# Convolution taps in a written order beside the query, key and value products of a first layer, on one core

## Chip, core and metric

The kernel runs on one core of one Trainium2 chip. The metric is the device time of one execution in microseconds (us), here the median of several runs; a profiled execution of its own gives the trace.

The engines are named as in the trace: PE is TensorE's matmul, PEld its load of weights, DVE is VectorE, ACT is ScalarE, POOL is GpSimd. DMAs are issued from SP's queue. Every engine works through its own list of instructions in order and waits on semaphores for the others.

## What is computed

The kernel is a chain of four transformer-like layers over 512 positions (and 256 context positions) of width 1024. Only the mixer of the first layer matters here. Cut to that:

```python
def conformer_conv(p_glu, conv_w, conv_b, ln_g, ln_b):
    a, gate = jnp.split(p_glu, 2, axis=-1)
    u = depthwise_conv(a * jax.nn.sigmoid(gate), conv_w, conv_b)   # 31 taps
    return jax.nn.silu(layer_norm(u, ln_g, ln_b))

def even_mixer(...):
    p_lat = h_lat @ w_in
    conv_lat = conformer_conv(p_lat[..., :EV_Q0], conv_w, conv_b, ln_g, ln_b)
    q_lat = apply_axial_rope(qk_heads(p_lat[..., EV_Q0:EV_K0]), rope)
    k_lat = apply_axial_rope(qk_heads(p_lat[..., EV_K0:EV_V0]), rope)
    v_lat = v_heads(p_lat[..., EV_V0:])
    ...
    o = lax.map(lambda qb: diff_attend(qb, k_all, v_all, lam), q_blocks)
    y_lat = jnp.concatenate([conv_lat, diff_merge(o, subln_g, lambda_init)], axis=-1) @ w_out
```

The same is done for the 256 context positions, with one set of weights. Beside it, this stage also computes rows of the modulation `c @ ada_w` for the first layer (kinds 2, 3 and 4) and, before, the filters of a later long convolution (the Hyena filters).

## The kernel before

Data lies with channels on the 128 partitions and positions along the free dimension; 768 columns are 512 latent and 256 context positions. Products run in three passes of rounded halves: `wsplit` (line 60) loads a weight of 128 x 1024 into a buffer `wraw`, ACT rounds it to `whi` (line 73), and a subtraction gives `wlo` (line 74), on VectorE or, where `eng` says so, on POOL. `mm3` (line 87) then adds hi x hi, hi x lo and lo x hi into one PSUM accumulator (lines 90 to 92). `whi` and `wlo` have two buffers each, `wraw` has three.

In `even_mixer` (line 355) the order is this. The input halves of the convolution are made in four channel blocks (`us`, lines 407 to 427), interleaved with the Hyena filters (`fg`). Then comes the stage of the change (lines 436 to 515): eight query and key products (line 489 on), each followed by a rope step of three VectorE passes (`stream_shuffle` line 494, lines 495 and 496) and an addition on POOL (line 497), then the values in two halves of six position tiles (line 501 on). Beside them run the taps of the 31-wide convolution (`taps`, line 437): per channel block 28 `scalar_tensor_tensor` passes of VectorE over 798 columns (line 449), two taps made by ACT (lines 443 and 446) and added on POOL into `o2` (line 447), and one addition of `o2` (line 452) on POOL. `conv_norm` (line 457) normalizes the result in two parts, latent and context. `taps` is a generator; the loops advance it with `next(tg)`.

`mods` (line 141) is a generator too: for each kind eight loads of `ada_w` into `wraw`, each with small products on TensorE (line 153), then a copy of the sum by ACT (line 157, it takes a `wraw` buffer as well) and a transposition (line 160). `behind` (line 168) makes every `wsplit` advance it by n steps, here 2.

Attention follows (line 540 on): 12 units of a head and a block of positions, with `scores` (line 558), `values` (line 590) and, as `filler` (line 623), one output product of the convolution half after each of the first eight units. The other half of the output products follows at the end (line 648).

The instructions of each engine are put in order when the kernel is built, by a planner that takes what is ready, the earlier in the program first; emission order therefore sets priorities and not the order itself. Buffers in one pool rotate; a pool that is opened on the memory of a closed one waits, tile by tile, for the last users of that memory. PSUM has eight banks: `evps` four, `evmps` (modulation) two and, after the filters' `evf` is closed, `evcps` (normalization) two. In attention `evaps`, `evop` and `evgp` lie on the banks of `evps`, and the scores' `evsp` on those of `evmps` and `evcps`.

Of the kernel before, what the change touches and what calls it, by code (L numbers as in the profile page):

```python
# [30 lines left out]
class K:  # L31
# [109 lines left out]
    def mods(self, l, kind, ps, pool=None, bufs=3):  # L141
# [6 lines left out]
        for kt in range(8):  # L148
            w = self.tmp([128, 1024], "wraw", bufs=bufs, pool=pool or self.wp)
            nc.sync.dma_start(out=w, in_=a["ada_w"][l, kt * 128:(kt + 1) * 128, kind * 1024:(kind + 1) * 1024])  # L150
            for hf in range(2):
                j = (kt % 2) * 2 + hf
                nc.tensor.matmul(acc[32 * j:32 * j + 32, :], self.cs[:, kt, :], w[:, hf * 512:(hf + 1) * 512],
                                 start=kt < 2, stop=kt >= 6)
            yield
# [199 lines left out]
def even_mixer(k, xc):  # L355
# [10 lines left out]
    with ExitStack() as es:  # L366
# [4 lines left out]
        mps = hp.enter_context(k.pool("evmps", 2, space=PSUM))  # L371
# [4 lines left out]
        with k.pool("hyf") as hy, k.pool("evf", 2, space=PSUM) as fps:  # L376
            fg = hyena_filters(k, fps, hy)
# [58 lines left out]
        with k.pool("evp") as pp, k.behind([k.mods(0, kind, mps) for kind in (2, 3, 4)], 2):  # L436
            def taps():

                for i in range(4):
# [8 lines left out]
                    for j in range(1, 29):  # L448
                        nc.vector.scalar_tensor_tensor(out=o, in0=u[:, j:j + W], scalar=cw[:, i, j:j + 1], in1=o, op0=ALU.mult, op1=ALU.add)
                        if j == 14:  # L450
                            yield
                    nc.gpsimd.tensor_tensor(out=o, in0=o, in1=o2, op=ALU.add)
# [33 lines left out]
            cps = hp.enter_context(k.pool("evcps", 2, space=PSUM))  # L486
            tg = taps()
            rope = k.cload("rope2d", [128, 2, T], pool=pp)
            for i in range(8):
                w = k.wsplit(a["ev_w_fm"][8 + i], eng=nc.gpsimd if i >= 4 else None)  # L490
                acc = k.gemm(w, h, 8, 0, T, ps)
                t1 = k.tmp([128, T], "rt1", bufs=1, pool=pp)
                t2 = k.tmp([128, T], "rt2", bufs=2, pool=pp)
                nc.vector.stream_shuffle(t2, acc, [(j + 16) % 32 for j in range(32)])
                nc.vector.tensor_tensor(out=t1, in0=acc, in1=rope[:, 0], op=ALU.mult)
                nc.vector.tensor_tensor(out=t2, in0=t2, in1=rope[:, 1], op=ALU.mult)
                nc.gpsimd.tensor_tensor(out=qk[i][:, 0:T], in0=t1, in1=t2, op=ALU.add)
                acc = k.gemm(w, h, 8, T, C, ps)
                nc.scalar.copy(qk[i][:, T:], acc)
                next(tg)  # L500
            for g in range(2):
                vb = [k.wsplit(a["ev_w_v"][g, kq * 4:kq * 4 + 4].rearrange("k p f -> p k f")) for kq in range(2)]
                for t in range(6):
                    acc = k.tmp([128, 512], "acc", pool=ps, bufs=None)[:, :256]
                    for kt in range(8):
                        s = slice(kt % 4 * 256, kt % 4 * 256 + 256)
                        w = vb[kt // 4]
                        k.mm3(acc, (hh[:, kt, t * 128:(t + 1) * 128], hl[:, kt, t * 128:(t + 1) * 128]),
                              (w[0][:, s], w[1][:, s]), kt == 0, kt == 7)
                    s = slice(g * 256, g * 256 + 256)  # L510
                    nc.scalar.copy(vv[:, t, s], acc)
                    if t % 3 == 2:
                        next(tg, None)
# [26 lines left out]
        with k.pool("eva") as pp, k.pool("evaps", 2, space=PSUM) as ps, k.pool("evop", 1, space=PSUM) as op_, k.pool("evgp", 1, space=PSUM) as gp, \  # L540
                k.pool("evsp", 2, space=PSUM) as sp:
# [81 lines left out]
            def filler(u):  # L623
                if u < 8:
                    out_gemm(0, [u], gp)
# [1625 lines left out]
```

## Time and profile before

| | |
|---|---|
| median of 3 runs | 3662.26 us (3659.52 to 3662.49) |
| profiled execution | 3663.87 us |
| its span, first to last instruction | 3662.1 us |
| PE busy | 3421.9 us (93%) |
| DVE busy | 2431.2 us (66%) |
| ACT busy | 1460.6 us (40%) |
| POOL busy | 665.8 us (18%) |

The stage of the change lies between about 170 and 360 us of the span, attention ends near 490. The shares are averages over the whole kernel; the stage differs from them, and it has to be read by itself. An engine's busy time counts what it executes, not whether anyone waits for it; the waits of PE show that. Matmul ends are modelled and overlap, so two matmuls in a row are best read by the distance of their starts.

### The profile page before, as it was taken

How to read it: one execution, taken by the hardware profiler on the slowest of the kernel's cores; microseconds unless marked ns; L12 is line 12 of the kernel's file. 1: busy time of each engine (PE TensorE's matmuls, PEld its weight loads, DVE VectorE, ACT ScalarE, POOL GpSimd, SP SyncE). 2: the span in 40 equal slices, each digit the busy share in tenths (PEclk: the TensorE clock that was granted, in tenths of full speed). 3: DMA queues.
4: the chain of work that ended last, by engine and by line, in shares of the span. 5: the costliest groups of instructions: out<-in, count | busy, mean ns of one | idle time of the engine just before them, and what ended most of it. 6: DMA issues, size and time to landing. Idle time of an engine off the chain costs nothing.

```text
span 3662.1 us, 54926 instructions
## 1 busy us (share of the span) xinstructions
PE 3421.9 (93%) x21924; PEld 2820.3 (77%) x21924; DVE 2431.2 (66%) x3995; ACT 1460.6 (40%) x2525; POOL 665.8 (18%) x587
## 2 busy tenths in 40 slices
PE   6987989999998899889999999999999999999999
PEld 3765878888887667667888877767998877777998
DVE  7997876544458765654334676657877676757886
ACT  4223543222226434323223444543444544644443
POOL 0042101102102332311111032021111032012110
PEclk9997999999999999889999999999999999999999
DMA  6334114333333222332223313232333313232333
GB/s 212 110 120 114 38 52 129 113 123 119 118 102 122 79 76 78 119 103 80 93 92 98 107 58 104 92 121 81 103 105 104 109 50 119 73 132 83 103 98 98
DMA packets 156842, 369.31 MB, mean 101 GB/s; under 512 B 19207, under 2 KB 44167, under 8 KB 156200
## 3 DMA queue, kind: packets, MB, share of 16 engines
q1 hardware_dynamic: 156584, 365.79, 31.5%
q8 instruction: 172, 2.82, 0.3%
q14 instruction: 86, 0.70, 0.1%
HBM read 334.27 MB, written 28.31 MB: 99 GB/s over the span
## 4 chain that ended last, share of the span: by engine, by line
PE 42%; DVE 12%; issue 6%; ACT 4%; POOL 2%; DMA 1%; SPq 0%; DVEq 0%; POOLq 0%; ACTq 0%
PE acc L90 12%; PE acc L92 12%; PE acc L91 12%; DVE wlo L74 1%; DMA wraw<-in_w_up_dram 1%; DVE hb L1614 1%; PE rec L1339 1%; PE rec L1340 1%; ACT whi L73 1%; DVE wslo L85 1%; PE acc L1416 1%; PE acc L1415 1%; DVE oz L830 1%; PE acc L1417 1%; ACT mp L1849 0%
## 5 line engine op out<-in xcount | busy, mean ns | idle before, releaser
L73 ACT CAST whi<-wraw 128x1024 fp32r<-128x1024 f32 (+2 forms) x442 | 408.0, 923 | 862.0 <-PE acc L91 664.4
L74 DVE TENSOR_TENSOR wlo<-wraw,whi 128x1024 fp32r<-128x1024 f32 (+2 forms) x438 | 487.1, 1112 | 185.4 <-ACT whi L73 180.7
L90 PE MATMUL acc<-hh,whi 128*128 128x512 f32 (+1 forms) x1024 | 367.4, 359 | 11.8 <-ACT whi L73 6.4
L92 PE MATMUL acc<-hh,wlo 128*128 128x512 f32 (+1 forms) x1024 | 364.9, 357 | 12.2 <-POOL wlo L74 8.8
L91 PE MATMUL acc<-hl,whi 128*128 128x512 f32 (+1 forms) x1024 | 365.8, 358 | 2.7 <-DVE hl L256 2.3
L91 PE MATMUL acc<-hidl,whi 128*128 128x512 f32 (+1 forms) x768 | 274.2, 357 | 1.6 <-DVE hidl L85 1.6
L92 PE MATMUL acc<-hidh,wlo 128*128 128x512 f32 (+1 forms) x768 | 274.2, 357 | 0.6 <-DVE wlo L74 0.6
L90 PE MATMUL acc<-hidh,whi 128*128 128x512 f32 (+1 forms) x768 | 274.4, 357 | 0.0
L341 POOL TENSOR_TENSOR sqr<-relu 128x512 f32<-128x512 f32 (+1 forms) x96 | 127.8, 1332 | 689.3 <-ACT relu L339 685.8
L90 PEld LDWEIGHTS acc<-hh,whi 128*128 128x128 f32 x1024 | 196.2, 192 | 50.9 <-ACT whi L73 10.2
L92 PEld LDWEIGHTS acc<-hh,wlo 128*128 128x128 f32 x1024 | 195.5, 191 | 47.0 <-POOL wlo L74 10.1
L91 PEld LDWEIGHTS acc<-hl,whi 128*128 128x128 f32 x1024 | 196.9, 192 | 35.4 <-DVE hl L256 5.9
L92 PE MATMUL acc<-shh,wlo 128*128 128x512 f32 (+1 forms) x480 | 194.7, 406 | 7.2 <-DVE wlo L74 7.2
L90 PE MATMUL acc<-shh,whi 128*128 128x512 f32 (+1 forms) x480 | 196.1, 409 | 3.5 <-ACT whi L73 3.5
L91 PE MATMUL acc<-shl,whi 128*128 128x512 f32 (+1 forms) x480 | 194.8, 406 | 1.1 <-issue 1.1
L85 POOL TENSOR_TENSOR flo<-fth,fhi 128x512 fp32r<-128x512 f32 x44 | 82.3, 1870 | 531.4 <-ACT fhi L84 506.5
L90 PE MATMUL acc<-fsh,wshi 128*128 128x256 f32 x576 | 163.7, 284 | 4.4 <-ACT wshi L84 4.4
L91 PEld LDWEIGHTS acc<-hidl,whi 128*128 128x128 f32 x768 | 145.1, 189 | 25.2 <-DVE hidl L85 2.0
L92 PE MATMUL acc<-fsh,wslo 128*128 128x256 f32 x576 | 162.5, 285 | 1.5 <-DVE wslo L85 1.5
L91 PE MATMUL acc<-fsl,wshi 128*128 128x256 f32 x576 | 163.4, 284 | 0.0
L92 PEld LDWEIGHTS acc<-hidh,wlo 128*128 128x128 f32 x768 | 144.3, 188 | 23.9 <-DVE wlo L74 1.0
L191 DVE SCALAR_TENSOR_TENSOR mdacc<-wraw,cs,mdacc 128x1024 f32<-128x1024 f32 x70 | 94.4, 1372 | 102.6 <-DMA wraw<-in_ada_w_dram 102.6
(684 smaller groups left out, 9142.8 us busy)
## 6 DMA issues: line engine op xcount, KB each, us to landing
wraw<-in_mlp_w_dram SPq DMA_DIRECT2D x128, 512.0 KB, 3.5
wraw<-in_ada_w_dram SPq DMA_DIRECT2D x96, 512.0 KB, 4.0
wraw<-in_w_in_dram SPq DMA_DIRECT2D x58, 512.0 KB, 3.5
wraw<-in_od_w_fm_dram SPq DMA_DIRECT2D x36, 512.0 KB, 3.6
wraw<-in_w_gate_dram SPq DMA_DIRECT2D x72, 256.0 KB, 2.9
wraw<-in_w_up_dram SPq DMA_DIRECT2D x72, 256.0 KB, 3.1
wraw<-in_w_down_dram SPq DMA_DIRECT2D x48, 256.0 KB, 2.7
wraw<-in_w_down_dram SPq DMA_DIRECT2D x32, 320.0 KB, 2.9
```

The lines of the kernel that those rows point to most:

```text
L73: nc.scalar.copy(hi, raw)
L74: (eng or nc.vector).tensor_tensor(out=lo, in0=raw, in1=f32(hi), op=ALU.subtract)
L85: (eng or nc.vector).tensor_tensor(out=lo, in0=src, in1=f32(hi), op=ALU.subtract)
L90: nc.tensor.matmul(out, s[0], m[0], start=first, stop=False)
L91: nc.tensor.matmul(out, s[0], m[1], start=False, stop=False)
L92: nc.tensor.matmul(out, s[1], m[0], start=False, stop=last)
L191: nc.vector.scalar_tensor_tensor(out=acc, in0=w, scalar=c, in1=acc, op0=ALU.mult, op1=ALU.add)
L341: nc.gpsimd.tensor_tensor(out=s, in0=r, in1=r, op=ALU.mult)
L830: nc.vector.scalar_tensor_tensor(out=o, in0=p[:, j:j + n], scalar=w[:, j:j + 1], in1=o, op0=ALU.mult, op1=ALU.add)
L1339: nc.tensor.matmul(op_[pf[d], hd], qd[:, c, pf[d]], S[:, c], start=True, stop=False)
L1340: nc.tensor.matmul(op_[pf[d], hd], at[pf[d], c], vn[pf[d], hd], start=False, stop=True)
L1415: nc.tensor.matmul(o, hh[:, kt, ts], w[0][:, ws], start=first, stop=False)
```

## The change

VectorE's instructions in the region of the query, key and value products are issued in the order in which the program emits them (`manual_schedule`); where they fall among VectorE instructions of outside the region, and the order of all other engines, stay the planner's. In the region, 40 steps of `taps` come first (a step is now a single tap, or the addition of `o2`), then the split of the first weight, and for each of the eight products: the next weight's split, five steps, the rope step. Each value tile is followed by three steps. All splits and the additions of `o2` are VectorE's. The normalization comes behind the region. Each `wsplit` advances the modulation by three steps, and three empty steps (`lag`) stand before each kind's copy. The PSUM pools change places: `evcps` is opened first and also serves the modulation before the filters' end, `evmps` is opened on the banks of `evf`; in attention `evsp` is on the banks of `evps`, `evgp` and `evop` on those of `evcps`, `evaps` on those of `evmps`. The convolution's output products come after units 2 to 9 in place of 0 to 7.

```diff
@@ -138,7 +138,7 @@
         nc.vector.tensor_reduce(out=self.sum4, in_=self.ident.rearrange("p (q j) -> p j q", q=4), axis=AX.X, op=ALU.add)
         self.md = {}
 
-    def mods(self, l, kind, ps, pool=None, bufs=3):
+    def mods(self, l, kind, ps, pool=None, bufs=3, lag=0):
 
 
 
@@ -152,6 +152,8 @@
                 j = (kt % 2) * 2 + hf
                 nc.tensor.matmul(acc[32 * j:32 * j + 32, :], self.cs[:, kt, :], w[:, hf * 512:(hf + 1) * 512],
                                  start=kt < 2, stop=kt >= 6)
+            yield
+        for _ in range(lag):
             yield
         row = self.tmp([128, 1024], "wraw", bufs=bufs, pool=pool or self.wp)[:, 0:512]
         nc.scalar.copy(row, acc)
@@ -368,12 +370,13 @@
         cp = es.enter_context(k.pool("evc"))
         tp_ = hp.enter_context(k.pool("evt", side="right"))
         ps = hp.enter_context(k.pool("evps", 4, space=PSUM))
-        mps = hp.enter_context(k.pool("evmps", 2, space=PSUM))
+        cps = hp.enter_context(k.pool("evcps", 2, space=PSUM))
         lam = cp.tile([128, 1], F32, name="lam")
 
         W = TC + 30
         conv = [k.tmp([128, W], "conv", F32, 4, cp) for i in range(4)]
         with k.pool("hyf") as hy, k.pool("evf", 2, space=PSUM) as fps:
+            mps = cps
             fg = hyena_filters(k, fps, hy)
             next(fg)
             xl = load_x()
@@ -433,7 +436,8 @@
             return k.tmp([128, TC], "b3", dt, 8, vp)
 
         qk = [b3() for i in range(8)]
-        with k.pool("evp") as pp, k.behind([k.mods(0, kind, mps) for kind in (2, 3, 4)], 2):
+        mps = hp.enter_context(k.pool("evmps", 2, space=PSUM))
+        with k.pool("evp") as pp, k.behind([k.mods(0, kind, mps, lag=3) for kind in (2, 3, 4)], 3):
             def taps():
 
                 for i in range(4):
@@ -447,9 +451,8 @@
                         nc.gpsimd.tensor_tensor(out=o2, in0=o2, in1=o3, op=ALU.add)
                     for j in range(1, 29):
                         nc.vector.scalar_tensor_tensor(out=o, in0=u[:, j:j + W], scalar=cw[:, i, j:j + 1], in1=o, op0=ALU.mult, op1=ALU.add)
-                        if j == 14:
-                            yield
-                    nc.gpsimd.tensor_tensor(out=o, in0=o, in1=o2, op=ALU.add)
+                        yield
+                    nc.vector.tensor_tensor(out=o, in0=o, in1=o2, op=ALU.add)
                     yield
                 for r in range(2):
                     yield from conv_norm(r)
@@ -483,34 +486,44 @@
                     nc.vector.scalar_tensor_tensor(out=cs[i], in0=th, scalar=1.0, in1=cs[i], op0=ALU.add, op1=ALU.mult)
                 yield
 
-            cps = hp.enter_context(k.pool("evcps", 2, space=PSUM))
             tg = taps()
             rope = k.cload("rope2d", [128, 2, T], pool=pp)
-            for i in range(8):
-                w = k.wsplit(a["ev_w_fm"][8 + i], eng=nc.gpsimd if i >= 4 else None)
-                acc = k.gemm(w, h, 8, 0, T, ps)
-                t1 = k.tmp([128, T], "rt1", bufs=1, pool=pp)
-                t2 = k.tmp([128, T], "rt2", bufs=2, pool=pp)
-                nc.vector.stream_shuffle(t2, acc, [(j + 16) % 32 for j in range(32)])
-                nc.vector.tensor_tensor(out=t1, in0=acc, in1=rope[:, 0], op=ALU.mult)
-                nc.vector.tensor_tensor(out=t2, in0=t2, in1=rope[:, 1], op=ALU.mult)
-                nc.gpsimd.tensor_tensor(out=qk[i][:, 0:T], in0=t1, in1=t2, op=ALU.add)
-                acc = k.gemm(w, h, 8, T, C, ps)
-                nc.scalar.copy(qk[i][:, T:], acc)
-                next(tg)
-            for g in range(2):
-                vb = [k.wsplit(a["ev_w_v"][g, kq * 4:kq * 4 + 4].rearrange("k p f -> p k f")) for kq in range(2)]
-                for t in range(6):
-                    acc = k.tmp([128, 512], "acc", pool=ps, bufs=None)[:, :256]
-                    for kt in range(8):
-                        s = slice(kt % 4 * 256, kt % 4 * 256 + 256)
-                        w = vb[kt // 4]
-                        k.mm3(acc, (hh[:, kt, t * 128:(t + 1) * 128], hl[:, kt, t * 128:(t + 1) * 128]),
-                              (w[0][:, s], w[1][:, s]), kt == 0, kt == 7)
-                    s = slice(g * 256, g * 256 + 256)
-                    nc.scalar.copy(vv[:, t, s], acc)
-                    if t % 3 == 2:
-                        next(tg, None)
+            def some(n):
+                for _ in range(n):
+                    next(tg, None)
+
+
+            with k.tc.manual_schedule(engines={mybir.EngineType.DVE}):
+                some(40)
+                w = k.wsplit(a["ev_w_fm"][8])
+                for i in range(8):
+                    accs = [k.gemm(w, h, 8, c0, n, ps) for c0, n in regs]
+                    if i < 7:
+                        w = k.wsplit(a["ev_w_fm"][9 + i])
+                    else:
+                        vb = [k.wsplit(a["ev_w_v"][0, kq * 4:kq * 4 + 4].rearrange("k p f -> p k f")) for kq in range(2)]
+                    some(5)
+                    acc = accs[0]
+                    t1 = k.tmp([128, T], "rt1", bufs=1, pool=pp)
+                    t2 = k.tmp([128, T], "rt2", bufs=2, pool=pp)
+                    nc.vector.stream_shuffle(t2, acc, [(j + 16) % 32 for j in range(32)])
+                    nc.vector.tensor_tensor(out=t1, in0=acc, in1=rope[:, 0], op=ALU.mult)
+                    nc.vector.tensor_tensor(out=t2, in0=t2, in1=rope[:, 1], op=ALU.mult)
+                    nc.gpsimd.tensor_tensor(out=qk[i][:, 0:T], in0=t1, in1=t2, op=ALU.add)
+                    nc.scalar.copy(qk[i][:, T:], accs[1])
+                for g in range(2):
+                    for t in range(6):
+                        acc = k.tmp([128, 512], "acc", pool=ps, bufs=None)[:, :256]
+                        for kt in range(8):
+                            s = slice(kt % 4 * 256, kt % 4 * 256 + 256)
+                            w = vb[kt // 4]
+                            k.mm3(acc, (hh[:, kt, t * 128:(t + 1) * 128], hl[:, kt, t * 128:(t + 1) * 128]),
+                                  (w[0][:, s], w[1][:, s]), kt == 0, kt == 7)
+                        s = slice(g * 256, g * 256 + 256)
+                        nc.scalar.copy(vv[:, t, s], acc)
+                        some(3)
+                    if g == 0:
+                        vb = [k.wsplit(a["ev_w_v"][1, kq * 4:kq * 4 + 4].rearrange("k p f -> p k f")) for kq in range(2)]
             for _ in tg:
                 pass
 
@@ -537,8 +550,8 @@
                     xs = x[r][:, m]
                     nc.vector.scalar_tensor_tensor(out=xs, in0=acc, scalar=k.mcol(0, 2, r)[:, m:m + 1], in1=xs, op0=ALU.mult, op1=ALU.add)
 
-        with k.pool("eva") as pp, k.pool("evaps", 2, space=PSUM) as ps, k.pool("evop", 1, space=PSUM) as op_, k.pool("evgp", 1, space=PSUM) as gp, \
-                k.pool("evsp", 2, space=PSUM) as sp:
+        with k.pool("eva") as pp, k.pool("evsp", 2, space=PSUM) as sp, k.pool("evgp", 1, space=PSUM) as gp, k.pool("evop", 1, space=PSUM) as op_, \
+                k.pool("evaps", 2, space=PSUM) as ps:
             def stack(hd):
 
                 QS = k.tmp([128, 2, TC], "QS", F32R, 2, pp)
@@ -621,8 +634,9 @@
                     k.split(o, hi[:, c0:c0 + n], lo[:, c0:c0 + n])
 
             def filler(u):
-                if u < 8:
-                    out_gemm(0, [u], gp)
+
+                if 2 <= u < 10:
+                    out_gemm(0, [u - 2], gp)
 
             sums = [pp.tile([128, 6], F32, name=f"esum{hd}") for hd in range(4)]
             mixt(4)
```

## Rows read from the trace of the kernel before

**Rows 1.** Busy us (instructions) of PE, PEld, DVE, ACT, POOL; PE clock, DMA.

```profile
240.00:300.00 60.00, 36.98 (x167) 23.20 (x166) 60.00 (x58) 6.20 (x9) 21.95 (x9) 0.74 0.31 97
300.00:360.00 60.00, 50.59 (x357) 44.12 (x356) 44.06 (x75) 28.29 (x55) 18.51 (x13) 0.87 0.45 128
```

**Rows 2.** Waits of PE, 190 to 360 us: total us, times, longest.

```profile
PE acc L92 <- POOL wlo L74: 8.8, 3, 8.3
PE acc L90 <- DVE rt L495: 7.9, 2, 5.7
...
PE acc L103 <- POOL cv L475: 5.3, 1, 5.3
```

**Rows 3.** DVE's groups, 80 to 360 us: count, busy us, mean ns, idle.

```profile
L449 DVE SCALAR_TENSOR_TENSOR conv<-xl,c_ev_conv_w,conv 128x798 f32<-128x798 f32 x112 | 136.0, 1253 | 0.4
L74 DVE TENSOR_TENSOR wlo<-wraw,whi 128x1024 fp32r<-128x1024 f32 x18 | 24.5, 1363 | 2.8 <-ACT whi L73 2.5 <-issue 0.3
...
L495 DVE TENSOR_TENSOR rt<-acc,c_rope2d 128x512 f32<-128x512 f32 x8 | 5.4, 678 | 0.5 <-POOL b L497 0.5
```

**Rows 4.** The same view of DVE, 172.2 to 191.3 us.

```profile
L449 DVE SCALAR_TENSOR_TENSOR conv<-xl,c_ev_conv_w,conv 128x798 f32<-128x798 f32 x6 | 6.2, 1039 | 0.0
...
L74 DVE TENSOR_TENSOR wlo<-wraw,whi 128x1024 fp32r<-128x1024 f32 x2 | 3.2, 1593 | 0.0
```

**Rows 5.** The same view of POOL, 80 to 360 us.

```profile
L497 POOL TENSOR_TENSOR b<-rt,rt 128x512 f32<-128x512 f32 x8 | 15.8, 1980 | 28.5 <-DVE rt L496 28.5
L74 POOL TENSOR_TENSOR wlo<-wraw,whi 128x1024 fp32r<-128x1024 f32 x4 | 11.3, 2813 | 4.0 <-ACT whi L73 4.0
...
L452 POOL TENSOR_TENSOR conv<-conv,cw 128x798 f32<-128x798 f32 x4 | 9.6, 2404 | 36.3 <-DVE conv L449 36.2
```

**Rows 6.** Timeline (start us, duration): the filters' last pass, the first `o2`.

```profile
191.30 0.68 DVE L726 TENSOR_TENSOR hyspec<-hys,hys 128x512 f32<-128x512 f32 x1
...
196.08 0.96 ACT L443 ACTIVATE cw<-xl,c_ev_conv_w 128x798 f32<-128x798 f32 x1
...
197.98 1.94 POOL L447 TENSOR_TENSOR cw<-cw,cw 128x798 f32<-128x798 f32 x1 [24.80 <-ACT cw L446]
```

**Rows 7.** Timeline of PE: the fifth product starts; the modulation follows it.

```profile
222.56 0.50 PE L90 MATMUL acc<-hh,whi 128*128 128x512 f32 x1
...
231.09 1.06 PE L153 MATMUL acc<-wraw,cs 128*32 128x512 f32 x8
```

**Rows 8.** Timelines of SP's queue and ACT: two weights issued and cast.

```profile
212.69 0.38 SPq L70 DMA_DIRECT2D wraw<-in_ev_w_fm_dram  x1
...
217.50 1.05 ACT L73 CAST whi<-wraw 128x1024 fp32r<-128x1024 f32 x1 [4.01 <-DMA wraw<-in_ev_w_fm_dram]
...
222.84 0.37 SPq L70 DMA_DIRECT2D wraw<-in_ev_w_fm_dram  x1
...
229.35 1.06 ACT L73 CAST whi<-wraw 128x1024 fp32r<-128x1024 f32 x1 [8.08 <-DMA wraw<-in_ev_w_fm_dram]
```

**Rows 9.** Timeline of DVE: twenty taps in a row.

```profile
268.28 20.32 DVE L449 SCALAR_TENSOR_TENSOR conv<-xl,c_ev_conv_w,conv 128x798 f32<-128x798 f32 x20
```

**Rows 10.** Timeline of ACT: copies of two value tiles in a row.

```profile
304.91 0.37 ACT L511 COPY vv<-acc 128x256 f32<-128x256 f32 x1 [1.62 <-PE acc L92]
307.62 0.37 ACT L511 COPY vv<-acc 128x256 f32<-128x256 f32 x1 [2.34 <-PE acc L92]
```

**Rows 11.** Timeline: normalization's first sum, second part's mean, last pass.

```profile
313.41 0.69 DVE L462 TENSOR_TENSOR cv<-cv,conv 128x512 f32<-128x512 f32 x1 [2.10 <-POOL conv L452]
...
342.36 0.50 PE L465 MATMUL acc<-ones,cv 128*128 128x1 f32 x4
...
357.56 0.75 DVE L483 SCALAR_TENSOR_TENSOR conv<-cv,conv 128x256 f32<-128x256 f32 x2
```

**Rows 12.** Timeline of PE: attention's first scores and first value product.

```profile
352.69 0.48 PE L571 MATMUL S<-KS,QS 128*128 128x512 f32 x1
...
375.47 2.76 PE L606 MATMUL acc<-pth,vv 128*128 128x256 f32 x12
```

## Prediction

> **What bounds the kernel now.** The change touches one stage of the first layer, so I read that stage and left the other 3300 us alone. First the busy time of each engine by stretches of 60 us [rows 1]: in 240 to 300 us VectorE is busy for all of the 60 us and TensorE for 37, at 0.74 of its clock. In the next stretch VectorE falls to 44 and TensorE is back at 51. So the reader is to see an engine (VectorE) that is full while TensorE waits for it, and then a stretch in which neither is full. Next, what TensorE waits for between 190 and 360 us [rows 2]: 8.8 us for a low half of a weight that POOL makes, 7.9 us until VectorE frees an accumulator in the rope step, 5.3 us for a sum of squares on POOL. None of these is a shortage of TensorE. Each is a short, urgent piece of work that stands behind something long and not urgent. Third, VectorE's own work, grouped [rows 3]: the 112 taps take 136.0 us, 1253 ns each, and nothing else there comes near it. Six taps that ran with POOL idle took 1039 ns each [rows 4], so (1253 - 1039) x 112 = 24 us of the taps is slowing by POOL.
>
> From these views: those three kinds of wait make 22 us, the lower clock beside them some more, the order on VectorE decides how much of it can be had, and a gain reaches the end only if attention, which follows, starts earlier.
>
> **The change part by part.**
>
> *Work moved between engines.* Four splits and four final additions leave POOL (11.3 and 9.6 us, [rows 5]) for VectorE. VectorE pays 4 x 1.2 us for the splits (the two of [rows 4] took 1.6 us under interference, the form's mean is 1.36 [rows 3]) and about 4 x 1.0 us for the additions (a two-operand pass over 512 columns takes 0.68 us [rows 3], 798 columns scale to 1.06): 9 us. It gets back part of the slowing: 24 us came with 15.8 + 11.3 + 9.6 us of POOL work [rows 5] and four L447 of at least 1.9 us [rows 6], 44 us together, so 0.54 us for each us on POOL, and 20.9 x 0.54 = 11.3 us. The exchange is worth 2 us at most on VectorE. Its bounds are 9 us lost (nothing given back) and 12 us won (all of it given back). The Trainium skill ("SBUF — State Buffer", section on the two separate sides) calls the port pair that both engines share an exclusive lock, the loser fully blocked. By that, all 20.9 us would come back; the rows show about half, and I go by the rows.
>
> *The order before the first query product.* The region gives VectorE one chain: 40 steps of the convolution, then the split of the first query weight. Where this chain lies among other work of VectorE is still free, so 28 taps of the first channel block can run early, as they do today. But step 29 is the addition of `o2`, and `o2` is built in tiles that lie on memory of the Hyena filters. Today the filters' last pass ends at 191.3 + 0.7 us, and `o2` is first scaled at 196.08 (0.96 us, twice), then added on POOL in 1.94 us [rows 6]. Steps 30 to 40 and the first split stand behind that. The filters themselves may end earlier, because 6 taps and 2 splits, 9.4 us, no longer stand between their passes [rows 4]; the bounds are 184 and 192 us, and I take 184, since on VectorE all of that work goes. Then 184 + 1.9 + 1.9 + 1.0 + 11 x 1.02 + 1.2 = 201 us until the first split is done. Until then TensorE can only load multipliers of the modulation. Today the splits of the first and of the second weight both lie before 191.3 [rows 4]. So the given order begins by losing some 10 us plus most of one product, and it has to earn that back.
>
> *Eight products for query and key.* One takes 231.09 - 222.56 = 8.5 us [rows 7], eight 68. VectorE has 1.2 (split) + 5 x 1.02 + 3 x 0.68 (rope) = 8.3 us for each, so it just keeps up, and the waits for a POOL split and for the rope step [rows 2] go. The modulation (3 steps for each weight now, where it was 2) of the first kind falls into the empty time before 201, that of the second costs five groups of 1.06 us [rows 7] and a transposition of about 1, some 6 us of TensorE. This comes to 201 + 68 + 6 = 275 us, if the weights are there.
>
> *Weights behind the modulation on the queue.* The weights and the modulation's operands share three `wraw` buffers. Today two operands and one weight make three: a weight takes the buffer of the weight before it. With three operands, a weight takes the buffer of the first operand of its own batch, and that one is used by TensorE only after the product before. Then the weight is loaded with nothing to cover it: 4.8 us from issue to cast in one row, 6.5 us in another [rows 8], plus 1.05 us for the cast, less 1 to 2 us of remaining operand work. I count 5 us for the weight of the fifth product (all later ones of that kind find their buffers freed in the pause) and 16.5 us for the two weights of the values, one after the other: two times (1 + 5 + 1.05 + 1.2), bounds 15.1 and 18.5 from the two rows. This is 275 + 5 + 16.5 = 296.5 us for the second split of the value weights. The nearest bound below is 2.3 us instead of 16.5 (cast and split alone), if the loads come in time.
>
> *The values.* Behind that split VectorE has 5 taps, a rope step, 18 taps, two splits, 18 taps: 41 x 1.02 [rows 9] + 2 + 2.4 = 46 us, until 343. TensorE's half of the values takes 6 x 2.7 = 16 us [rows 10], so it stands idle for about 10 us before the second half, whose weights wait behind 18 taps, and it ends with VectorE, near 341.
>
> *The normalization of the convolution.* Today it runs between the value products, from 313.4 to 358.3 us [rows 11]. In the new order all of it stands behind the last tap. Its second half alone, 256 columns, took 342.4 to 358.3, 16 us; the first half has double the columns on POOL and VectorE, so I take 22 us for both in overlap, between 16 and the 45 of today.
>
> *Output products two units later, PSUM pools in another order.* Scores go to the four banks that the products leave, so they don't wait for the normalization any more. The two units without output products fill the time of the normalization. But the pools of the attention output and of the output products get the normalization's two banks, so the first value product of attention waits for its last read: 343 + 22 = 365 us. Today it starts at 375.5, 23 us after the first scores [rows 12]. That is 10.5 us earlier. One output product that is done before 375 today is done later (half of 8.5 us, so 4), and two of them now stand at the end of the stage, where TensorE has holes; I take 3 us back.
>
> The sum: 10.5 - 4 + 3 = 9.5 us less than the profiled execution's 3663.9 us (3662.1 us of span and 1.8 us around it), 3654.4. The profiled execution lies 1.6 us above the median of the three timed ones, so the forecast for a median is 3653 us.
>
> **The rivals.**
>
> *The loads come in time.* The planner may put an operand's product into a gap of TensorE, and then the buffer is free early. Then 5 and 14 us of load waits go, and the whole chain after them with them: 9.5 + 19 = 28.5 us less, 3634 us. For it: TensorE has gaps at each split. Against it: today's operands are used only after the product, though they landed long before.
>
> *The order costs what it gives.* If the filters end at 192 as today, the start is 8 us later, and if the sixth weight waits like the fifth, 5 us more: 9.5 - 13 makes 3.5 us more than today, 3666 us. VectorE then has idle time in front of splits that it never had.
>
> *Slower: the normalization becomes the bound.* The place is the two PSUM banks, the price is the length of that chain. If it takes the 45 us that it takes now [rows 11], because POOL and VectorE also prepare attention's operands then, it costs 23 us more than I count: 3676 us. From 39 us on (22 + 9.5 + 7.3) the kernel is slower by what can be told.
>
> *The region doesn't bind.* It could be that the planner's own order was the same where it matters. Speaks against it: the waits of [rows 2] are all of an order that the region excludes. I give it no chance of its own; it would end within the third case's "no change".
>
> **How the numbers follow.** About 0.2%, 7.3 us, is what a measurement of this kernel can tell from no change. Forecast 3653 us (3645 to 3660 by its own terms): 0.36. Loads in time, 3634: 0.22. Gives back what it wins, 3666: 0.25. Normalization as bound, 3676: 0.17. Faster: all of the second case and 0.8 of the first, 0.51. Same: the third and the rest of the first, 0.32. Slower: 0.17. The range has to take in the second case and most of the fourth: 3631 to 3672.
>
> **What would show it.** In the profile after: (1) the first L449 after the addition at about 189, and the first query split near 201; (2) no POOL L74 or L452 in the stage, taps near 1.1 us each; (3) ACT's cast of the fifth key or query weight and of both value weights waiting for DMA, with TensorE idle for 5 us in front; (4) about 10 us of TensorE idle in the middle of the values, ended by a VectorE split; (5) the last tap near 343; (6) the first L606 some 22 us after it, waiting for the normalization. Wrong would be: the first split before 195 (then `o2` wasn't in the way), no load waits (second case), or a first L606 after 375, which makes it slower. If the median is below 3640 us, my chain on VectorE was not the bound.

## The result, and the profile after

The changed kernel takes 3718.29 us (median of four runs, 3710.80 to 3723.03), the kernel before 3662.38. The ratio is 1.0150, with a 95% interval from 1.0137 to 1.0163: slower by some 55 us, where I had forecast 3653 us and a range up to 3672. The profiled execution of after took 3718.78 us, with a span of 3717.0.

All of it is lost in the stage that I had read. The end of the stage is seen best at ScalarE's first square for the norm that follows. The first row is of the kernel before, the second of the kernel after (timelines: start, duration, instruction, and in brackets the idle time before it with what ended it):

```profile
494.88 0.63 ACT L222 ACTIVATE nsq<-xl 128x512 f32<-128x512 f32 x1 [2.22 <-DVE xl L538]
```

```profile
552.79 0.63 ACT L224 ACTIVATE nsq<-xl 128x512 f32<-128x512 f32 x1 [2.22 <-DVE xl L551]
```

That is 57.9 us later; the spans differ by 54.9. Inside the stage, the busy time of the engines, answering to [rows 1] and one stretch further (PE, PEld, DVE, ACT, POOL, then the granted clock):

```profile
240.00:300.00 60.00, 51.99 (x257) 38.68 (x256) 41.66 (x50) 7.23 (x10) 8.20 (x5) 0.89 0.36 122
300.00:360.00 60.00, 43.47 (x295) 34.76 (x294) 43.59 (x48) 8.51 (x15) 3.31 (x2) 0.83 0.29 93
360.00:420.00 60.00, 32.41 (x154) 27.76 (x153) 50.73 (x85) 29.69 (x56) 15.73 (x12) 0.66 0.26 70
```

VectorE, which was full at 240 to 300 us, now has a third of its time free, and TensorE has holes in every stretch. The bound of before is gone and no engine took its place: this is a stage in which each waits for another. What TensorE waits for from 190 to 360 us, answering to [rows 2] (total, times, longest):

```profile
PE acc L90 <- ACT whi L73: 20.7, 5, 4.7
PE acc L91 <- DVE wlo L74: 12.2, 1, 12.2
```

Of the three kinds of wait that I had wanted to see go, the first two are gone, 16.7 us. The third, for POOL's sum of squares, has only moved behind 360 us together with the normalization: two waits of 12.3 us there, for 5.3 before. In the place of the two stand 20.7 us for weights not yet cast (two waits before the first product runs, two in front of later products, one in front of the values) and 12.2 us for one split. The work itself moved as I had said: POOL has no split and no final addition any more, and a tap costs 1118 ns instead of 1253 (groups of DVE and of POOL, 80 to 360 us, answering to [rows 3, 5]).

```profile
L453 DVE SCALAR_TENSOR_TENSOR conv<-xl,c_ev_conv_w,conv 128x798 f32<-128x798 f32 x105 | 117.4, 1118 | 2.7
```

```profile
L512 POOL TENSOR_TENSOR b<-rt,rt 128x512 f32<-128x512 f32 x8 | 11.9, 1489 | 101.3 <-DVE rt L511 101.3
L451 POOL TENSOR_TENSOR cw<-cw,cw 128x798 f32<-128x798 f32 x4 | 9.3, 2321 | 33.4 <-ACT cw L450 21.2 <-ACT cw L447 11.1 <-DVE conv L455 1.1
```

**The start**, answering to [rows 4, 6]: a wait of SP's queue (183.9 to 185.9 us), then timelines of SP's queue, ACT, POOL and DVE.

```profile
SPq L70 <- PE acc L153: 1.6, 1, 1.6
185.48 0.33 SPq L70 DMA_DIRECT2D wraw<-in_ev_w_fm_dram  x1
...
189.91 1.04 ACT L73 CAST whi<-wraw 128x1024 fp32r<-128x1024 f32 x1 [10.94 <-DMA wraw<-in_ev_w_fm_dram]
190.86 0.96 ACT L447 ACTIVATE cw<-xl,c_ev_conv_w 128x798 f32<-128x798 f32 x1
...
192.80 1.88 POOL L451 TENSOR_TENSOR cw<-cw,cw 128x798 f32<-128x798 f32 x1 [20.10 <-ACT cw L450]
195.75 2.64 POOL L451 TENSOR_TENSOR cw<-cw,cw 128x798 f32<-128x798 f32 x1 [1.07 <-DVE conv L455]
199.46 2.58 POOL L451 TENSOR_TENSOR cw<-cw,cw 128x798 f32<-128x798 f32 x1 [1.07 <-ACT cw L450]
...
194.71 0.99 DVE L455 TENSOR_TENSOR conv<-conv,cw 128x798 f32<-128x798 f32 x1 [8.35 <-POOL cw L451]
195.62 14.87 DVE L453 SCALAR_TENSOR_TENSOR conv<-xl,c_ev_conv_w,conv 128x798 f32<-128x798 f32 x11
210.40 2.35 DVE L74 TENSOR_TENSOR wlo<-wraw,whi 128x1024 fp32r<-128x1024 f32 x2
212.67 5.38 DVE L453 SCALAR_TENSOR_TENSOR conv<-xl,c_ev_conv_w,conv 128x798 f32<-128x798 f32 x5
```

The filters' last pass on VectorE ends at 186.4 us, near my 184. But on ScalarE the cast of the first query weight stands in front of the scaling of `o2`; that weight is issued at 185.48, when TensorE has used the modulation's operand that held its buffer, and so `o2` is scaled 4.5 us after the filters' end. The eleven taps behind its addition then take 14.87 us instead of 11.2, beside POOL's next additions. The first split is done at 211.6 us (210.40 and half of the 2.35), not at 201.

**The products and their weights**, answering to [rows 7, 8]: the stretches of the fifth, sixth and seventh product, the first matmuls of the fifth and sixth, and four casts on ACT.

```profile
254.40:265.60 11.20, 11.16 (x52) 8.84 (x56) 10.19 (x11) 0.96 (x1) 3.04 (x2) 0.77 0.22 69
271.30:282.50 11.20, 11.16 (x52) 8.87 (x54) 11.06 (x12) 1.05 (x1) 2.14 (x1) 0.76 0.23 82
283.50:292.20 8.70, 8.70 (x55) 7.62 (x51) 5.30 (x8) 1.66 (x3) 1.29 (x1) 1.00 0.34 121
```

```profile
254.38 0.80 PE L90 MATMUL acc<-hh,whi 128*128 128x512 f32 x1 [4.11 <-ACT whi L73]
271.25 0.79 PE L90 MATMUL acc<-hh,whi 128*128 128x512 f32 x1 [3.82 <-ACT whi L73]
...
253.28 1.05 ACT L73 CAST whi<-wraw 128x1024 fp32r<-128x1024 f32 x1 [4.44 <-DMA wraw<-in_ev_w_fm_dram]
270.15 1.04 ACT L73 CAST whi<-wraw 128x1024 fp32r<-128x1024 f32 x1 [4.16 <-DMA wraw<-in_ev_w_fm_dram]
...
307.42 1.04 ACT L73 CAST whi<-wraw 128x1024 fp32r<-128x1024 f32 x1 [4.45 <-DMA wraw<-in_ev_w_v_dram]
317.01 1.05 ACT L73 CAST whi<-wraw 128x1024 fp32r<-128x1024 f32 x1 [8.54 <-DMA wraw<-in_ev_w_v_dram]
```

Two key or query weights come late with TensorE idle in front, not one, and a product behind such a pause takes 11.2 us at a mean granted clock of 0.77 or 0.76 (part of it at the lower of the two levels, 1.2 GHz), where the one at full clock takes 8.7.

**The values**, answering to [rows 9, 10]: DVE, then PE.

```profile
336.26 10.81 DVE L453 SCALAR_TENSOR_TENSOR conv<-xl,c_ev_conv_w,conv 128x798 f32<-128x798 f32 x10
346.99 1.22 DVE L74 TENSOR_TENSOR wlo<-wraw,whi 128x1024 fp32r<-128x1024 f32 x1
...
348.26 0.58 PE L91 MATMUL acc<-wlo,hh 128*128 128x256 f32 x1 [12.25 <-DVE wlo L74]
```

**The normalization and attention's start**, answering to [rows 11, 12]: DVE, PE and POOL, ordered by engine.

```profile
369.80 0.69 DVE L465 TENSOR_TENSOR cv<-cv,conv 128x512 f32<-128x512 f32 x1
407.84 1.66 DVE L482 SCALAR_TENSOR_TENSOR conv<-acc,c_ev_ln,conv 128x256 f32<-128x256 f32 x4
412.47 0.42 DVE L486 SCALAR_TENSOR_TENSOR conv<-cv,conv 128x256 f32<-128x256 f32 x1
...
379.78 0.77 PE L584 MATMUL S<-KS,QS 128*128 128x512 f32 x1 [0.65 <-DMA KS<-KS]
387.76 1.87 PE L103 MATMUL acc<-ones,cv 128*128 128x1 f32 x8 [7.22 <-POOL cv L478]
421.01 0.70 PE L619 MATMUL acc<-pth,vv 128*128 128x256 f32 x2 [0.47 <-DVE mx L589]
...
383.64 4.07 POOL L478 TENSOR_TENSOR cv<-cv,cv 128x512 f32<-128x512 f32 x3 [3.93 <-ACT cv L476]
```

The last tap ends at 368.3 us and the normalization at 412.9. TensorE issues its first score at 379.78 and then stands 7.2 us before a sum of squares that POOL has not finished, with the next scores behind it. VectorE's last reads of the normalization's PSUM banks (L482) end at 409.5, 11.5 us before the first value product at 421.01.

### The profile page after: what moved, and what is told of

It reads as the page before. It is cut to its first block, busy times and chain, and to the rows that moved or that the text cites. A ratio compares the mean times of both kernels' runs of the same rounds, so it can differ in the third digit from the quotient of the medians.

```text
span 3717.0 us, 54928 instructions
## 1 busy us (share of the span) xinstructions
PE 3437.2 (92%) x21924; PEld 2832.3 (76%) x21924; DVE 2434.2 (65%) x4003; ACT 1463.9 (39%) x2525; POOL 639.5 (17%) x579
## 4 chain that ended last, share of the span: by engine, by line
PE 40%; DVE 13%; issue 6%; ACT 4%; POOL 2%; DMA 2%; SPq 0%; DVEq 0%; ACTq 0%; POOLq 0%
PE acc L90 11%; PE acc L92 11%; PE acc L91 11%; DVE wlo L74 2%; DMA wraw<-in_w_up_dram 1%; DVE wslo L85 1%; DVE hb L1628 1%; PE acc L1429 1%; PE rec L1353 1%; PE acc L1430 1%; ACT whi L73 1%; PE rec L1354 1%; PE acc L1431 1%; DVE ws L1936 1%; PE rec L1338 1%
## 5 line engine op out<-in xcount | busy, mean ns | idle before, releaser
L90 PEld LDWEIGHTS acc<-hidh,whi 128*128 128x128 f32 x768 | 144.8, 189 | 23.3
```

Of the source, the lines that this page charges most:

```text
L90: nc.tensor.matmul(out, s[0], m[0], start=first, stop=False)
```

## The experiments

Ratios are to the kernel before, from the same comparison; its median was 3658.6 to 3663.7 us in them, so two rows are best compared by their ratios. "Stage end" is the row shown first above (before 494.9, after 552.8).

| kernel | us | ratio, 95% interval | stage end |
|---|---|---|---|
| e1 after, no region | 3679.1 | 1.0042 (1.0027 to 1.0056) | 515.4 |
| e2 after, two operands per weight | 3689.0 | 1.0069 (1.0054 to 1.0084) | 527.5 |
| e3 after, first split earlier | 3704.4 | 1.0110 (1.0095 to 1.0125) | 540.7 |
| e4 after, early output products | 3713.0 | 1.0147 (1.0132 to 1.0162) | 544.5 |
| e5 after, own buffers | 3682.1 | 1.0046 (1.0029 to 1.0063) | 517.7 |
| e6 after, no normalization | 3706.6 | 1.0130 (1.0115 to 1.0145) | 525.9 |
| e7 before, no normalization | 3653.8 | 0.9987 (0.9977 to 0.9996) | 478.0 |
| e8 before, own buffers | 3661.8 | 1.0007 (0.9994 to 1.0020) | 500.2 |
| e9 after, eight taps | 3726.8 | 1.0185 (1.0168 to 1.0202) | 560.6 |
| e10 = e3 + e5 + e9 | 3708.5 | 1.0141 (1.0125 to 1.0157) | 543.4 |
| e11 = e10, no region | 3657.2 | 0.9993 (0.9984 to 1.0003) | 494.0 |
| e12 before, late output products | 3664.1 | 1.0017 (1.0006 to 1.0028) | 501.5 |
| e13 = e10, normalization behind a split | 3685.9 | 1.0062 (1.0045 to 1.0079) | 522.5 |
| e14 = e11, early output products | 3653.6 | 0.9981 (0.9971 to 0.9990) | 488.8 |
| e15 after, own buffers, no region | 3657.9 | 0.9995 (0.9985 to 1.0005) | 494.1 |

### e1: the region alone undone

```diff
-            with k.tc.manual_schedule(engines={mybir.EngineType.DVE}):
+            if True:
```

> The kernel after without the region that fixes VectorE's order; all else as in after. Theory A (the given order itself costs: between 180 and 360 us VectorE is only 40 us busy in each 60, because taps stand behind splits that wait for their weights): the taps fill those holes again, the last one ends some 20 us earlier than 368, and the time falls to about 3695 us. Theory B (the weights come late because three operands of the modulation pass through the same buffers, whoever orders VectorE): within 5 us of 3718.

39 us came back, more than A had said. VectorE's busy time in one stretch, the end of its taps and what followed on TensorE:

```profile
240.00:300.00 60.00, 51.85 (x289) 38.70 (x290) 59.79 (x67) 8.32 (x12) 12.54 (x6) 0.95 0.40 138
```

```profile
306.79 0.99 DVE L455 TENSOR_TENSOR conv<-conv,cw 128x798 f32<-128x798 f32 x1
...
331.69 0.95 PE L468 MATMUL acc<-ones,cv 128*128 128x1 f32 x8
351.36 1.87 PE L103 MATMUL acc<-ones,cv 128*128 128x1 f32 x8 [5.50 <-POOL cv L478]
```

VectorE fills its holes again and is done with the taps 61 us earlier, at 306.8. The weights still come late (TensorE waits 17.2 us for casts), but the taps no longer wait with them. The normalization doesn't use the lead: its steps were emitted behind all value products, and TensorE takes the first of them only at 331.7 us, 22 us after VectorE had it ready, and the sum of squares at 351.4.

### e2 and e5: the weights' buffers

e2 goes back to two steps of the modulation per weight, without the empty steps. e5 keeps three and gives the operands buffers of their own:

```diff
-[k.mods(0, kind, mps, lag=3) for kind in (2, 3, 4)], 3)
+[k.mods(0, kind, mps) for kind in (2, 3, 4)], 2)            # e2
+[k.mods(0, kind, mps, pp, 4, lag=3) for kind in (2, 3, 4)], 3)   # e5
```

> The kernel after with two steps of the modulation for each weight and no empty steps before its last copy, as in the kernel before. Theory B (late weights): the waits of ScalarE's casts for weights, 3 x 4 us for query and key and 8.5 us for the values, go, and the products of query and key take 74 us instead of 90: about 3695 us. Theory A (the order): the weights then wait for something else, 5 us at most are won, 3713.

> The kernel after with the modulation's operands of this stage in four buffers of their own, so that the three buffers of the weights hold weights alone. Theory B: no cast of the stage waits for its weight, the eight products take 74 us instead of 90 and the values' two weights come without a wait, 25 us less, 3693 us. Theory A: the casts come earlier, but the splits still stand behind taps; 8 us less at most, 3710.

29 and 36 us came back, so B held as well. Its sign held only in part in e2: ScalarE's casts still wait there for landing weights (43.5 us from 190 to 345 us, as many as in after), but TensorE waits 2.2 us for a cast where it waited 20.7. In e5 ScalarE's waits in front of a weight's cast end with TensorE alone (190 to 345 us):

```profile
ACT whi L73 <- PE acc L91: 65.2, 8, 11.6
```

But for 2.1 us, also ended by TensorE, that is the whole of them: no cast waits for a landing weight any more. The start gains by it too: `o2` is scaled at 186.06 us in e5, 4.8 us earlier than in after.

### e3: the first split in front of `o2`

```diff
-                some(40)
+                some(28)
                 w = k.wsplit(a["ev_w_fm"][8])
+                some(12)
```

> The kernel after with the split of the first query weight behind 28 steps of the convolution instead of 40, so that it no longer stands behind the addition of o2. By my account of the start (ScalarE's cast waits for the weight until 189.9, o2 is scaled behind it, first split done at 211.6 instead of 201): the first split is done before 195, and 12 to 17 us of it reach the end, 3704 us. Rival: the weights' loads pace the products anyway, the products start earlier and wait more: within 4 us of 3718.

3704.4: as expected, 14 us arrive at the end. The first split starts at 190.0 us, 20 us earlier, and the stage ends 12 us earlier.

### e8: the same buffers in the kernel before

```diff
-k.behind([k.mods(0, kind, mps) for kind in (2, 3, 4)], 2)
+k.behind([k.mods(0, kind, mps, pp, 4) for kind in (2, 3, 4)], 2)
```

> The kernel before with the modulation's operands of this stage in four buffers of their own. Theory B: in the kernel before, ScalarE's casts wait for weights too (8.1, 8.0, 9.4 and 8.2 us of its idle time end with a landing weight), so late weights cost there as well: 8 us less, 3655 us. Rival (there POOL's splits and VectorE's taps set the pace, as my reading of before said): within 3 us of 3663.

No difference that can be measured: ScalarE's waits for weights cost nothing of note there. That is not yet the price of late weights in after, because in before a weight follows two operands and in after three; e1 and e15 show that price without the region.

### e6 and e7: the normalization left out

Both leave out these lines and compute attention's mixture from the sum without it:

```diff
-                for r in range(2):
-                    yield from conv_norm(r)
```

> The kernel after with the convolution's normalization left out (both halves; attention and the output products work on the unnormalized sum). Theory C (the normalization is a chain of about 45 us that begins at the last tap and whose end sets the end of the stage, some 133 us later): it goes, the next bound is the last value product at 366.6 plus the 138 us that the stage before takes from its first scores, 40 us less, 3678 us. Rival (attention starts late by itself, and the normalization lies beside it): 10 us less at most, 3708.

> The kernel before with the same normalization left out. Theory C: there it lies beside the value products, which end at 350.5 while it ends at 358.3, so only some 8 us of it and what it takes from the values' engines are seen: 3650 to 3657 us. Rival: it costs about as much in either kernel, 3624 us.

The first rows behind the stage (e6, then e7):

```profile
525.94 0.63 ACT L224 ACTIVATE nsq<-xl 128x512 f32<-128x512 f32 x1 [2.22 <-DVE xl L549]
```

```profile
478.04 0.63 ACT L222 ACTIVATE nsq<-xl 128x512 f32<-128x512 f32 x1 [2.22 <-DVE xl L536]
```

The stage ends 26.9 us earlier without it in after and 16.8 us in before, so 10 us of the stage's delay are normalization that lies open. The totals fell less, because what follows the stage took longer in both (10 and 8 us by the spans), which leaves 16.5 and 9.2 us; why was not looked into. By the totals e6 sides with the rival, by the stage it lies between the two theories: some 45 us of chain, 27 of them exposed. The total of e7 fits theory C, but its stage shows twice the 8 us that C had.

### e4 and e12: the output products two units later

```diff
-                if 2 <= u < 10:
-                    out_gemm(0, [u - 2], gp)
+                if u < 8:
+                    out_gemm(0, [u], gp)         # e4; e12 the reverse, in before
```

> The kernel after with the output products of the convolution's half in the units 0 to 7 as before, instead of 2 to 9. Theory C (the end of the normalization sets the end of the stage): the first product can't start before the normalization is done in either case, and stands in front of other work then: 3715 to 3725. Rival (the two units later leave TensorE short of work at the front and push two products to the end): 10 us less, 3708.

> The kernel before with the output products of the convolution's half in units 2 to 9 instead of 0 to 7, all else as before. By my sum this part costs 1 us (4 lost, 3 won back): 3664. If TensorE has nothing else at the start of attention, where one product of 8.5 us ran before the first value product: 5 to 9 us more, 3670.

In after the ratio hardly moves (1.0147 for 1.0150), though the stage ends 8 us earlier. In before the later products cost 0.17% (0.06 to 0.28%), some 6 us, as the second expectation said; the medians alone differ by 3.5 us, so the size is loose.

### e9 and e10: more taps beside each product

e9 is one edit; e10 adds those of e3 and e5.

```diff
-                    some(5)
+                    some(8)
```

> The kernel after with eight steps of the convolution beside each query or key product instead of five, so that the taps end inside the values and the normalization's steps lie between the value products again. Theory D (the given order puts too few taps beside products that leave VectorE a third idle, and so pushes the last tap, the second value weights and the normalization back): the last tap ends near 330 instead of 368, the normalization lies beside the values, 25 us less, 3693 us. Rival (late weights alone pace the stage, VectorE only waits with it): the taps end earlier, the values don't, 5 us less at most, 3713.

> The kernel after with three edits together: own buffers for the modulation's operands, the first query split behind 28 steps, eight steps beside each product. If the three places where after loses time (the start, the late weights, the late taps with the normalization behind them) are all of it, their gains (36, 14 and about 20 us of the 55, less what they share) bring it to the kernel before: 3650 to 3665 us. If attention also loses by the later output products or by the order of the PSUM pools, it stays 8 to 12 us above before, 3672.

Theory D fell: e9 is slower than after, although its last tap ends 29 us earlier. And e10, which was to end at 3672 us at most, loses 26 us against e5 (35 by the ratios). DVE and PE of e10 show where:

```profile
294.82 3.43 DVE L74 TENSOR_TENSOR wlo<-wraw,whi 128x1024 fp32r<-128x1024 f32 x2
...
308.55 12.82 DVE L453 SCALAR_TENSOR_TENSOR conv<-xl,c_ev_conv_w,conv 128x798 f32<-128x798 f32 x11
...
379.33 1.22 DVE L74 TENSOR_TENSOR wlo<-wraw,whi 128x1024 fp32r<-128x1024 f32 x1
...
380.60 0.58 PE L91 MATMUL acc<-wlo,hh 128*128 128x256 f32 x1 [9.25 <-DVE wlo L74]
```

The taps end at 321, inside the first half of the values. The steps that are emitted next are the normalization's, all in front of the split for the second half. In a fixed order that split then waits for the whole chain, until 379.3, and TensorE's second half with it.

### e11 and e13: the same edits without the region, and with another order in it

e11 is e10 with e1's edit. e13 is e10 with this one:

```diff
-                        some(3)
+                        some(1 if g else 2)
```

> The same three edits, and VectorE's order not fixed. If the given order is harmless once the weights and the taps come in time: the same as with it, within 5 us. If the order costs by itself (a split that waits holds the taps behind it): 8 to 15 us less than with it.

> The three edits with the given order kept, and only the normalization's steps put behind the split of the second half's value weights: two taps instead of three behind each of the first six value products, one step behind each of the last six. Theory E (the given order costs where something late and long stands in front of a split that TensorE waits for): the second half begins near 325 instead of 380, the values end near 345, what is left is the normalization in its strict order, 3670 to 3680 us. Rival (the order costs everywhere, by many small waits): 3700 or more.

e11 takes 3657.2 us where e10 takes 3708.5: the same work, 51 us apart, where 8 to 15 had been expected. In e11 the second half's splits lie between taps:

```profile
304.05 1.22 DVE L74 TENSOR_TENSOR wlo<-wraw,whi 128x1024 fp32r<-128x1024 f32 x1
305.18 1.04 DVE L453 SCALAR_TENSOR_TENSOR conv<-xl,c_ev_conv_w,conv 128x798 f32<-128x798 f32 x1
306.26 1.05 DVE L453 SCALAR_TENSOR_TENSOR conv<-xl,c_ev_conv_w,conv 128x798 f32<-128x798 f32 x1
307.23 1.22 DVE L74 TENSOR_TENSOR wlo<-wraw,whi 128x1024 fp32r<-128x1024 f32 x1
```

e13 keeps the region and splits at 326.5 instead of 379.3. It gets back 23 of the 51 us (29 by the ratios), a little less than E had said; its values end at 362, not 345. So one place in the order costs 23 to 29 us. What the rest goes to has no run of its own; TensorE's largest two waits in e13 (190 to 420 us) are still for VectorE:

```profile
PE acc L91 <- DVE wlo L74: 9.8, 2, 8.5
PE acc L90 <- DVE rt L511: 7.7, 4, 2.9
```

### e14 and e15: what is left

e14 is e11 with e4's edit, e15 is after with the edits of e1 and e5.

> The kernel after with the modulation's operands in buffers of their own and no region; the taps as in after. The two edits gave 36 and 39 us alone. Two causes that add up would give 3650 or less; one cause seen from two sides (a late weight costs because the order holds everything behind its split) 3660 to 3675.

> The three edits, no region, and the output products in units 0 to 7 as in the kernel before. In the kernel before, two units later cost 0.17%, so the same step back gives some 5 us: 3651, which is 0.2% under before. If attention starts late enough that the products don't matter: 3657 as without this edit.

e15: some 60 us together, where 39 and 36 came singly, so about 15 us of the two are one and the same loss; that lies between the two expectations. Buffers of their own are worth 21 us where the order is free (e1 to e15; 17 by the ratios) and 36 in the given order (after to e5). With the region and the late weights gone, all that was lost is back: e15 can't be told from the kernel before. e14 is faster than both kernels, by 0.19% against before (0.10 to 0.29%). Of the change it keeps the splits and additions on VectorE, three operands per weight and the pools' order; it drops the given order and the later output products, and adds the edits of e10.

## Why the prediction was wrong, link by link

My sum was one chain. Here each link's forecast stands beside what the trace has; the last column is what the link added by itself.

| point | forecast | after | late by | new |
|---|---|---|---|---|
| first query split done | 201 | 211.6 | 10.6 | 10.6 |
| eighth product done | 280 | 302.5 | 22.5 | 11.9 |
| second value weight split | 296.5 | 319.3 | 22.8 | 0.3 |
| last tap | 343 | 368.3 | 25.3 | 2.5 |
| normalization done | 365 | 412.9 | 47.9 | 22.6 |
| attention's first value product | 365 | 421.0 | 56.0 | 8.1 |
| stage end (494.9 - 9.5) | 485.4 | 552.8 | 67.4 | 11.4 |

**Right**: the work moved off POOL; the late weight behind three operands, and the load waits of both value weights (16.8 us for my 16.5, with some luck: they took 7.2 and 9.6 where I had counted 8.25 for each, and my bounds of 15.1 and 18.5 don't follow from that term); the hole of 12 us in the middle of the values, ended by a VectorE split (10 forecast); the length of VectorE's chain behind it (49 us for 46). The sign that I had named for "slower", a first value product after 375, came.

**The order before the first query product.** I put the scaling of `o2` directly behind the filters. ScalarE runs in order too, and a cast that waits for a late load stood in front, 4.5 us; the taps beside POOL's next additions took another 3.7 us more than I had counted. The filters' end itself was off by 2.4 us (192.0 less 9.4 is 182.6, where I wrote 184). e3 shows the price of having the split behind `o2` at all: 14 us.

**Weights behind the modulation.** I counted one late weight among the products; two came with TensorE idle, 4.1 and 3.8 us, and I gave no price to the clock behind a pause, 2.5 us for each such product. Together that is 12.9 us where I had 5, so 8 of the 11.9 us. I had priced "the sixth weight waits like the fifth" in a rival, as an alternative.

**The normalization.** This term of the sum is the largest error. I took 22 us "in overlap", nearer to the lower bound of 16 than to the 45 of before. It took 44.6. The 16 us were counted from the second half's mean; its sums lay in front of that, beside other work, and its steps wait for one another on four engines, so two halves don't shorten it. The rival had it at 45 us and gave 3676: right in the price, and the forecast should have been built on it. But the place that the rival and my sum both name, the two PSUM banks, was not what attention waited for last: they were read for the last time at 409.5 us, and the first value product came at 421.0. Between them lie attention's own steps, on the same VectorE and ScalarE as the end of the normalization. Left out, it sets free 27 us of the stage in after and 17 in before (e6, e7). An open normalization need not make the kernel slower: in e15, which loses nothing, attention takes 40.5 us from its first scores to its first value product, nearly as in after (41.2; before 22.8), but its values end at 322.8 us, 28 us ahead of those of before.

**Output products.** From attention's first value product to the stage's end I had counted 1 us more than before; it took 12.4 more (131.8 for 119.4). e12 measures some 6 us (2 to 10) for this part alone; the rest has no run of its own.

**The deeper fault** is in how the rivals were made. A late start together with a late sixth weight, and the normalization as the bound, were alternatives with chances of their own, each on top of an otherwise punctual chain. They were links of the same chain, and in a fixed order they added up: 10.6, 11.9 and 22.6 us on one bill, the first of them from another cause than I had named, since the filters ended at 186.4 and not at 192. The runs show the mechanism. Against the kernel before, late weights with the order free lose 15 us (e1), the given order with the weights in time 18 (e5), and both together 55, 22 more than the sum of the two; with neither, nothing is lost (e15).

Not settled: the pools' order in PSUM was not tried alone, nor was the exchange between POOL and VectorE.

## What to carry to other kernels

An order written out by hand for an engine is only as good as the latest input in it: each instruction that may wait makes everything behind it wait, on ScalarE and in TensorE's queue too, so go through the order and ask of each split, cast and sum when its input really lands. When you cost such a chain, take for each link the whole time that a trace shows for it, count on an overlap only where a row shows it, and don't offer the delays of its links as alternatives: they add. Before fixing an order, give the loads buffers of their own; then try whether the order is still wanted.

## What the runs showed of the hardware

A pause costs twice: two products behind pauses of 4 us took 11.2 us at a mean granted clock of 0.76 and 0.77, the same product without a pause 8.7 at 1.00. From 360 to 420 us, with TensorE busy for 32.4 of 60 us, the clock stood at 0.66.

POOL and VectorE take turns. POOL's first addition into `o2`, beside an idle VectorE, took 1.88 us; the next two, beside taps, took 2.64 and 2.58. Beside each of these two, one of the eleven taps took 2.53 us:

```profile
196.70 2.53 DVE L453 SCALAR_TENSOR_TENSOR conv<-xl,c_ev_conv_w,conv 128x798 f32<-128x798 f32 x1
200.35 2.53 DVE L453 SCALAR_TENSOR_TENSOR conv<-xl,c_ev_conv_w,conv 128x798 f32<-128x798 f32 x1
```

The other nine took 1.04 to 1.05. Both slow taps end 0.85 us after POOL's pass (199.23 after 198.39, 202.89 after 202.04), so they stood nearly still until it ended, and POOL's pass, 0.7 to 0.8 us longer than the first, stood behind the tap in front of it. The Trainium skill ("SBUF — State Buffer", section on the two separate sides) has the loser fully blocked; these rows agree with it. The eleven taps lost 3.0 us (14.87 for 11 times 1.08) while POOL was busy for 5.2, or 0.57, near the 0.54 that I had used; but the share is that low because POOL's busy time holds its own waiting. My "about half" was therefore no argument against the page.
